# Operand placement in a two-layer encoder trunk: activations at one residue of 256 bytes, pair weights eight bytes further up, full-height decay products

## The chip, the core and the metric

The kernel runs on one core of a Trainium2 chip. The metric is device time in microseconds for one execution of the whole program, the median over several runs. A core has a matrix engine (TensorE, PE in the profile, with its weight loads listed apart as PEld), a vector engine (VectorE, DVE), an activation engine (ScalarE, ACT), a general engine (GpSimd, POOL), a queue engine (SyncE, SP), and 16 DMA engines that all queues share. Operands of a matrix product lie in SBUF, which has 128 partitions. A tile has the same byte address in each partition that it covers. This document is about those byte addresses, taken modulo 256.

## The reference

`x` is 512 frames by 1024 features, and there are two layers. One layer computes:

```
h = rmsnorm(x);  z = h @ w_in + b_in          # 12296 columns, split into parts
A: mLSTM, 4 heads:  s = (q k^T) * exp(log decay between frames), causal;  num = s @ v
   y_m = sigmoid(o) * head_norm(num / denominator)
B: retention, 4 heads:  s = (rope(q) rope(k)^T) * gamma^(distance), causal;  num = s @ v
   y_r = silu(g) * head_norm(num)
x += (sigmoid(gm) * (y_m @ w_bm) + sigmoid(gr) * (y_r @ w_br)) @ w_out
x += relu(rmsnorm(x) @ w_ff1 + b_ff1)^2 @ w_ff2 + b_ff2
x += sigmoid(rmsnorm(x) @ w_pe_gate) * (p @ w_pe)
```

A last rmsnorm ends the program. All of it is float32.

## The kernel before

Every float32 operand is held as two parts of TensorE's `float32r` type, a high and a low one, and a product is three matmuls into one accumulator: high by high, high by low, low by high (`mm3`, line 479). ScalarE writes the high part (line 303) and VectorE the low one (line 304); `split` does both. One matmul has 128 weight columns held in the array and streams 256 or 512 columns of the other operand past them. The text calls the streamed one the moving operand and the other the stationary one.

The work is cut into units, one list per layer (`unit_list`, line 171). Weights stream in with one DMA per unit or part of it, are split two pieces ahead of their use (`prep_next`, line 425; `LOOK`), and rotate through a pool `w`. There are three kinds of large unit.

- A T8 unit (`t8`, line 484): eight 128-row blocks of weights, stationary, against 512 columns of activations, 24 matmuls.
- A PAIR unit (`run_pair`, line 512): two output tiles by a fast 2x2 block scheme with seven products instead of eight. Each product is 12 matmuls of 256 moving columns at lines 531 to 533, so a unit has 84. Its weights are four pieces, A to D. Three of the seven moving operands are the activations themselves, four are sums of them, made ahead (`xs` from line 1329 for the mixing half of a layer, `ns` for the first feed-forward matrix). For the second feed-forward matrix all seven come from the `hid` tiles `h`. There are 75 PAIR units, so 6300 such matmuls: 32 units read `hid`, 28 read activations and `xs`, 15 read activations and `ns`.
- A WIDE unit (`run_wide`, line 549): the same scheme with the roles exchanged: weights are the moving operand, 512 columns, and activations or `xs` are stationary, at lines 575 to 577. There are eight, with 168 matmuls each; four sevenths of them, 768, have `xs` stationary.

The last seventh product of a PAIR unit (P4) is put off into the next unit (`later`, `flush`). The framework orders instructions on each engine by a priority and its own cost estimate, so rows of neighbouring products may interleave.

Where a tile lies is set by pools. `cpool` holds constants, among them `bc`, all bias and gain columns of both layers, loaded at the start. `pad` and the `shift` tiles (line 275) only take room, so that later tiles lie further up. With them, in the built program, all stationary weights begin at byte 224 of 256, and so do most activations; `xs`, `hid` and the operand `pt` begin at byte 32. One operand differs by head: an mLSTM value tile holds two heads of 258 columns, so in `attend` (line 830) the even heads' moving operand begins at byte 224 and the odd heads' at 232, against stationary operands at 224 for both. Each weight part, high and low, is a tile of its own, two tiles per piece (line 437).

The decay matrix of an mLSTM head starts from a product `rp` (line 1062): a selector `sel` and the gate rows `grows`, both 36 partitions high, spread one row over 128 partitions. There is one per head and layer, eight in all.

Of the kernel before, what the change touches and what calls it, by code (L numbers as in the profile page):

```python
# [35 lines left out]
F32 = mybir.dt.float32  # L36
F32R = mybir.dt.float32r
AF = mybir.ActivationFunctionType
OP = mybir.AluOpType
# [3 lines left out]
P = 128  # L43
T = 512
NT = T // P
D = 1024
KT = D // P
L = 2
H = 4
# [9 lines left out]
PIECES = 3  # L59
PAD = 48  # L60
LAST = 4
# [16 lines left out]

# [174 lines left out]
def build(ctx, tc, ins, out):  # L253
    nc = tc.nc
# [170 lines left out]
    def prep_next():  # L425
# [229 lines left out]
    class Norm:  # L655
# [10 lines left out]
        def col(self, k):  # L666
            o, _ = _B[self.gain]
            return bc[:, self.i, o + k:o + k + 1]

# [89 lines left out]
    def bcol(i, n, k):  # L759
        o, _ = _B[n]  # L760
        return bc[:, i, o + k:o + k + 1]

# [114 lines left out]
    def gate_rows(i, o, nrm):  # L877
# [42 lines left out]
        x = 0  # L920
# [42 lines left out]
    fill_raws(2)  # L963
    nc.scalar.dma_start(bc[:, 0, 8:NB], ins["vecs"][0][:, 8:NB])
    for k in range(1, KT):
# [6 lines left out]
    nc.sync.dma_start(ident, ins["ident"])  # L972
    nc.sync.dma_start(bc[:, 1, :], ins["vecs"][1])

    for i in range(L):
# [7 lines left out]

        sel = cur["br"].tile([P, H, P], F32R, name=f"l{i}sel", tag="sel")[0:32 + H]
        t = tmp(f"l{i}selraw")
        gp.memset(t[0:32 + H, :], 0.0)
        for r in (0, 32):
            nc.sync.dma_start(t[r:r + H, :T], ins["sel"])
        ve.tensor_copy(sel.rearrange("k h p -> k (h p)"), t[0:32 + H, :T])
        x_src = ins["xT"] if i == 0 else xs_dram  # L990
# [3 lines left out]
        negb = cols.tile([P, 16], F32, name=f"l{i}negb", tag="negb")  # L994
        gp.tensor_scalar(negb, bc[:, i, ob:ob + 16], -1.0, None, OP.mult)
        cbp = cols.tile([P, 16], F32, name=f"l{i}cbp", tag="cbp")
        gp.tensor_tensor(cbp, bc[:, i, ow:ow + 16], bc[:, i, ow + 16:ow + 32], OP.add)
        for j in (2, 3):
            gp.tensor_tensor(cbp, cbp, bc[:, i, ow + 16 * j:ow + 16 * j + 16], OP.add)
        gp.tensor_tensor(cbp, cbp, bc[:, i, ob:ob + 16], OP.mult)  # L1000
        gp.tensor_tensor(cbp, cbp, bc[:, i, oc:oc + 16], OP.add)

        fix = cols.tile([P, 3, 16], F32, name=f"l{i}fix", tag="fix", bufs=1)
        for j in range(3):
            gp.tensor_tensor(fix[:, 2 - j, :], bc[:, i, ow + 16 * j:ow + 16 * j + 16], negb, OP.mult)
            if j:
                gp.tensor_tensor(fix[:, 2 - j, :], fix[:, 2 - j, :], fix[:, 3 - j, :], OP.add)
# [16 lines left out]
        def conv_evac(o, nm, c, qh, ql, q, nrm):  # L1024
            a = tmp(f"{nm}cv")
            cw = [bc[:, i, ow + 16 * j + c:ow + 16 * j + c + 1] for j in range(4)]
            if nrm:
# [435 lines left out]
        for c in range(KT):  # L1463
# [118 lines left out]
        embed(1)  # L1582
        shift(cur["ff"], ph_side, False)
        cur["ff"].release()
# [142 lines left out]
def _pack_vecs(a):  # L1727
    v = np.zeros((L, P, NB), np.float32)
    for i in range(L):
        def put(n, x, off=0):  # L1730
            o, _ = _B[n]
            x = x.reshape(-1, P).T
            v[i, :, o + off:o + off + x.shape[1]] = x
# [11 lines left out]
        put("brk", b[CRK:CRK + 1024])  # L1745
        put("brg", b[CRG:CRG + 2048])
        put("bgm", b[CGM:CGM + 1024])
# [53 lines left out]
```

## Time and profile before

| what | value |
|---|---|
| median of three runs | 2320.76 us (lowest 2318.07) |
| the profiled execution: its span | 2313.4 us |
| outside the span, from the median | 7.4 us |
| PE busy | 2299.1 us, 13532 matmuls |
| PEld busy | 2035.4 us |
| DVE busy | 1766.8 us |
| ACT busy | 1269.6 us |
| POOL busy | 624.1 us |
| DMA | 499.36 MB, mean busy share by the page's rows about 0.8 |

The page gives busy time per engine. Matmuls are pipelined: one lasts longer in the record than the distance to the next, so a busy PE can still be slower than it need be. The measure that matters here is the spacing, the distance from one matmul's start to the next one's. It is read from the timeline, whose first column is the start in microseconds, the second the duration of one, and then the engine, the line, the operation, output<-inputs, and the shapes. The page's times are of one execution; the median is of others.

### The profile page before, as it was taken

The page shows a single profiled execution, that of the slowest core. Times are in us where ns is not written, and L with a number is a line of the kernel's source. Part 1 is how long each engine was busy: PE and PEld are TensorE (multiplying, and loading weights), DVE is VectorE, ACT ScalarE, POOL GpSimd, SP SyncE. Part 2 cuts the span into 40 slices and gives each one's busy share as a digit, 9 for nine tenths or more (in the row PEclk, how much of TensorE's full clock was granted, in tenths as well). Part 3 has the DMA queues.
Part 4 walks back from the last instruction along what each step waited for, and adds up shares of the span by engine and source line. Part 5 has one row for each costly group of instructions (what it writes and reads, how often), then busy time and mean ns, then how long its engine had stood idle before and what let it go on. Part 6 is the DMA issues. An engine that isn't in the chain of part 4 may idle for free.

```text
span 2313.4 us, 36468 instructions
## 1 busy us (share of the span) xinstructions
PE 2299.1 (99%) x13532; PEld 2035.4 (88%) x13532; DVE 1766.8 (76%) x2690; ACT 1269.6 (55%) x1837; POOL 624.1 (27%) x984
## 2 busy tenths in 40 slices
PE   9999999999999999999999999999999999999998
PEld 8888899888898899999888888988888888999997
DVE  7878767886676878788778777778867678787785
ACT  6756544644554546556557564445445446566564
POOL 4333222223124322223442332221231242111112
PEclk9999999999999999999999999999999999999999
DMA  7776787777789888888886768877877898878851
GB/s 218 189 191 174 238 228 216 215 227 210 232 230 261 220 228 223 240 239 215 222 224 182 196 174 247 232 216 216 223 221 208 241 266 218 247 232 228 232 160 55
DMA packets 187603, 499.36 MB, mean 216 GB/s; under 512 B 26064, under 2 KB 29520, under 8 KB 187424
## 3 DMA queue, kind: packets, MB, share of 16 engines
q0 software_dynamic: 57520, 188.53, 37.1%
q1 hardware_dynamic: 114496, 281.06, 36.6%
q10 hardware_dynamic: 15408, 27.43, 3.5%
q8 instruction: 106, 1.74, 0.3%
q14 instruction: 73, 0.60, 0.1%
HBM read 478.05 MB, written 194.51 MB: 291 GB/s over the span
## 4 chain that ended last, share of the span: by engine, by line
PE 92%; DVE 5%; ACT 1%; issue 1%; DMA 1%; POOL 0%; SPq 0%; ACTq 0%; DVEq 0%; POOLq 0%
PE l0br L480 1%; PE l1br L480 1%; PE l1br L481 1%; PE l0br L482 1%; PE l1br L482 1%; PE l0br L481 1%; PE l0f L480 1%; PE l0f L481 1%; PE l0f L482 1%; PE l1f L480 1%; PE l1f L481 1%; PE l1f L482 1%; PE l0pg L480 1%; PE l1bm L480 1%; PE l0pg L482 1%
## 5 line engine op out<-in xcount | busy, mean ns | idle before, releaser
L303 ACT ACTIVATE wh<-wr 128x1024 fp32r<-128x1024 f32 (+1 forms) x193 | 199.7, 1041 | 140.5 <-issue 17.1
L304 DVE TENSOR_TENSOR wl<-wr,wh 128x1024 fp32r<-128x1024 f32 (+1 forms) x191 | 234.6, 1230 | 37.5 <-ACT wh L303 36.9
L303 ACT ACTIVATE wh_B<-wr 128x1024 fp32r<-128x1024 f32 x123 | 130.3, 1059 | 184.5 <-PE l0br L481 15.7
L304 DVE TENSOR_TENSOR wl_B<-wr,wh_B 128x1024 fp32r<-128x1024 f32 x123 | 150.3, 1222 | 55.1 <-ACT wh_B L303 50.6
L303 ACT ACTIVATE wh_C<-wr 128x1024 fp32r<-128x1024 f32 x75 | 79.2, 1056 | 69.5 <-PE l0br L481 8.3
L304 DVE TENSOR_TENSOR wl_C<-wr,wh_C 128x1024 fp32r<-128x1024 f32 x75 | 91.7, 1223 | 21.3 <-ACT wh_C L303 17.1
L303 ACT ACTIVATE wh_A<-wr 128x1024 fp32r<-128x1024 f32 x75 | 78.9, 1052 | 44.3 <-DMA wr<-wpairs 5.2
L304 DVE TENSOR_TENSOR wl_A<-wr,wh_A 128x1024 fp32r<-128x1024 f32 x75 | 91.6, 1221 | 12.6 <-ACT wh_A L303 9.4
L303 ACT ACTIVATE wh_D<-wr 128x512 fp32r<-128x512 f32 x75 | 47.2, 630 | 96.5 <-DVE wr L462 27.3
L303 ACT ACTIVATE wh_t<-wr 128x1024 fp32r<-128x1024 f32 x56 | 59.4, 1061 | 69.0 <-PE l0g2va L576 6.0
L304 DVE TENSOR_TENSOR wl_t<-wr,wh_t 128x1024 fp32r<-128x1024 f32 x56 | 68.2, 1221 | 26.1 <-ACT wh_t L303 25.5
L304 DVE TENSOR_TENSOR wl_D<-wr,wh_D 128x512 fp32r<-128x512 f32 x75 | 51.8, 690 | 30.2 <-ACT wh_D L303 28.7
L480 PE MATMUL l0f<-l0n2h,wh 128*128 128x512 f32 x176 | 68.7, 390 | 0.0
L481 PE MATMUL l0f<-l0n2l,wh 128*128 128x512 f32 x176 | 68.6, 390 | 0.0
L482 PE MATMUL l0f<-l0n2h,wl 128*128 128x512 f32 x176 | 68.5, 389 | 0.0
L361 POOL DMA_DIRECT2D s30t<-wpairs x24 | 16.8, 699 | 92.4 <-PE l1o11a L533 9.4
L482 PEld LDWEIGHTS l0f<-l0n2h,wl 128*128 128x128 f32 x176 | 33.0, 188 | 7.0
L480 PEld LDWEIGHTS l0f<-l0n2h,wh 128*128 128x128 f32 x176 | 33.1, 188 | 6.6
L481 PEld LDWEIGHTS l0f<-l0n2l,wh 128*128 128x128 f32 x176 | 33.1, 188 | 6.5
L480 PE MATMUL l1f<-l1n2h,wh 128*128 128x512 f32 x96 | 37.6, 391 | 0.0
L481 PE MATMUL l1f<-l1n2l,wh 128*128 128x512 f32 x96 | 37.5, 390 | 0.0
L482 PE MATMUL l1f<-l1n2h,wl 128*128 128x512 f32 x96 | 37.4, 389 | 0.0
(5797 smaller groups left out, 9132.4 us busy)
## 6 DMA issues: line engine op xcount, KB each, us to landing
wr<-wstream SPq DMA_DIRECT2D x189, 512.0 KB, 4.8
wr<-wpairs SPq DMA_DIRECT2D x225, 256.0 KB, 4.1
wr<-wwide SPq DMA_DIRECT2D x48, 512.0 KB, 4.7
s3t<-wwide POOLq DMA_DIRECT2D x24, 256.0 KB, 5.0
s6t<-wwide POOLq DMA_DIRECT2D x24, 256.0 KB, 5.0
s18t<-wwide POOLq DMA_DIRECT2D x24, 256.0 KB, 4.7
s21t<-wwide POOLq DMA_DIRECT2D x24, 256.0 KB, 5.3
s24t<-wpairs POOLq DMA_DIRECT2D x24, 256.0 KB, 5.7
```

The costliest lines, as they stand in the source:

```text
L303: a = ac.activation(hi_ap, src, AF.Copy)
L304: return a, ve.tensor_sub(lo_ap, src, hi_ap.bitcast(F32))
L361: dma = gp.dma_start(piece(g, x, p, q), piece(g, MADE[x][a], p, q), max_dma_last_dim=4096, **kw)
L480: te.matmul(o, sh, mh, start=first, stop=False)
L481: te.matmul(o, sh, ml, start=False, stop=False)
L482: cur["mm"] = te.matmul(o, sl, mh, start=False, stop=last)
```

## The change

- `bc` keeps only the columns that are needed outside the branches (72 per layer instead of 249; the unused `brg` goes). The branch columns, 161 per layer, are a tile `bcl` loaded per layer by `branch_cols`: for layer 0 at the start, for layer 1 after the output projection of layer 0, both from ACT's queue.
- The `shift` tiles go. In the built program all moving and stationary activations, `xs`, `hid` and `pt` among them, now begin at byte 224.
- High and low part of a weight piece are slices of one tile, 64 columns longer than the two. In PAIR units, and in the four last units (whose matmuls have 256 columns), both parts begin two columns, 8 bytes, further in: at byte 232. The others stay at 224.
- `sel` and the gate rows are used at 128 partitions, with zeros below row 36, so `rp` is a 128-row product.

Number and shape of matmuls are otherwise the same.

```diff
-for _n, _c in (("g1", 8), ("g2", 8), ("g3", 8), ("gf", 8), ("bqk", 16), ("cw", 64), ("cb", 16), ("bo", 8),
-               ("brq", 8), ("brk", 8), ("brg", 16), ("bgm", 8), ("bgr", 8), ("bf1", 32), ("bf2", 8),
-               ("gmn", 8), ("grn", 16), ("bif", 1)):
+for _n, _c in (("g1", 8), ("g2", 8), ("g3", 8), ("gf", 8), ("bf1", 32), ("bf2", 8), ("bqk", 16), ("cw", 64), ("cb", 16),
+               ("bo", 8), ("brq", 8), ("brk", 8), ("bgm", 8), ("bgr", 8), ("gmn", 8), ("grn", 16), ("bif", 1)):
...
+NK = _B["bqk"][0]
+SLACK = 64
...
-    def shift(pl, side, start):
-
-        if (side == "left") == start:
-            pl.tile([P, 16 if start else 48], F32, name="shift", tag="shift")
...
-    bc = cpool.tile([P, L, NB], F32, name="bc")
+    bc = cpool.tile([P, L, NK], F32, name="bc")
     nc.scalar.dma_start(bc[:, 0, 0:8], ins["vecs"][0][:, 0:8])
+    bcl = {}
+
+    def branch_cols(i):
+
+        bcl[i] = cpool.tile([P, NB - NK], F32, name=f"bc{i}", tag="bcl")
+        nc.scalar.dma_start(bcl[i], ins["vecs"][i][:, NK:NB])
+
+    def bvec(i, o, n=1):
+        return bc[:, i, o:o + n] if o < NK else bcl[i][:, o - NK:o - NK + n]
...
-        kw = {"tag": "d", "bufs": 2} if x == "D" else {"tag": "l", "bufs": 2 * LAST} if pl is not wpool else {
-            "tag": "w", "bufs": 2 * PIECES}
+        kw = {"tag": "d", "bufs": 1} if x == "D" else {"tag": "l", "bufs": LAST} if pl is not wpool else {
+            "tag": "w", "bufs": PIECES}
...
-        out_ = [pl.tile([P, w], F32R, name=f"w{a}{n}_{nm}", **kw) for a in ("h" if gates else "hl")]
+        both = pl.tile([P, 2 * w + SLACK], F32R, name=f"w{n}_{nm}", **kw)
+        o = 2 if units[n][0] == "PAIR" or pl is not wpool else 0
+        out_ = [both[:, o + a * w:o + a * w + w] for a in range(1 if gates else 2)]
...
-        rr = cur["br"].tile([P, T], F32R, name=n + "rr", tag="rr")[0:32 + H]
+        rr = cur["br"].tile([P, T], F32R, name=n + "rr", tag="rr")
...
-    nc.scalar.dma_start(bc[:, 0, 8:NB], ins["vecs"][0][:, 8:NB])
+    nc.scalar.dma_start(bc[:, 0, 8:NK], ins["vecs"][0][:, 8:NK])
+    branch_cols(0)
...
-        sel = cur["br"].tile([P, H, P], F32R, name=f"l{i}sel", tag="sel")[0:32 + H]
+        sel = cur["br"].tile([P, H, P], F32R, name=f"l{i}sel", tag="sel")
...
-        shift(xs_pool, act_side, True)
         xs_t = acts(xs_pool, f"l{i}xs")
-        shift(xs_pool, act_side, False)
...
         cur["low"].release()
+        if i == 0:
+            branch_cols(1)
...
-        shift(cur["ff"], ph_side, True)
```

The framework also puts some rows in another order. On PE, at the gates of layer 0 after the first rope products, the old order ran the first matmul of the next product (output bank `l0bgm2b`) inside the product before it (`l0bgm2a`). `wh_B` and `wl_B` are the two parts of one weight piece, the same piece that is `w_B` now.

```order
L533 MATMUL l0r0brka<-l0xnh_1348,wl_D 128x256
L531 MATMUL l0bgm2a<-l0xsh_1373,wh_B 128x256
L532 MATMUL l0bgm2a<-l0xsl_1374,wh_B 128x256
L531 MATMUL l0bgm2b<-l0xnh_1059,wh_B 128x256
L533 MATMUL l0bgm2a<-l0xsh_1373,wl_B 128x256
```

Now, from the same place:

```order
L541 MATMUL l0r0brka<-l0xnh_1331,w_D 128x256
L539 MATMUL l0bgm2a<-l0xsh_1356,w_B 128x256
L540 MATMUL l0bgm2a<-l0xsl_1357,w_B 128x256
L541 MATMUL l0bgm2a<-l0xsh_1356,w_B 128x256
L539 MATMUL l0bgm2a<-l0xsh_1360,w_B 128x256
```

The matmul that reads the low part (line 533, now 541) moves one place forward, and the borrowed matmul goes back into its own product.

On POOL, the derived convolution columns of layer 1 (`l1negb`, `l1cbp`, `l1fix`) stood near the program's start, since `bc` held both layers:

```order
L1000 TENSOR_TENSOR l0cbp<-l0cbp,bc 128x16
L1001 TENSOR_TENSOR l0cbp<-l0cbp,bc 128x16
L995 TENSOR_SCALAR l1negb<-bc 128x16
L997 TENSOR_TENSOR l1cbp<-bc 128x16
L999 TENSOR_TENSOR l1cbp<-l1cbp,bc 128x16 x2
```

Now they stand at the end of layer 0's mixing half, among the DMAs that fetch `x` again and those that make the weight sums `s10t` for the second feed-forward matrix:

```order
L1453 DMA l0x_7212<-xT 128x512
L367 DMA s10t_120<-wpairs 64x1024
L1004 TENSOR_SCALAR l1negb<-bc_7621 128x16
L1006 TENSOR_TENSOR l1cbp<-bc_7621 128x16
L1014 TENSOR_TENSOR l1fix<-bc_7621,l1negb 128x16 x2
L1008 TENSOR_TENSOR l1cbp<-l1cbp,bc_7621 128x16
```

There `l1negb` waits until the second load of branch columns has landed, and the weight sums behind it wait with it.

More of the change, by code (lines that the diff above doesn't have):

```diff
@@ L667, in col @@
             o, _ = _B[self.gain]
-            return bc[:, self.i, o + k:o + k + 1]
+            return bvec(self.i, o + k)
         def tile(self, k, x):
@@ L760, in bcol @@
         o, _ = _B[n]
-        return bc[:, i, o + k:o + k + 1]
+        return bvec(i, o + k)
     def rows_split_v(i, h, nm, n_, j, o, rc, bvt, vh, vl):
@@ L972, in build @@
     nc.sync.dma_start(ident, ins["ident"])
-    nc.sync.dma_start(bc[:, 1, :], ins["vecs"][1])
+    nc.sync.dma_start(bc[:, 1, :], ins["vecs"][1][:, 0:NK])
     for i in range(L):
@@ L994, in build @@
         negb = cols.tile([P, 16], F32, name=f"l{i}negb", tag="negb")
[L995 removed]
+        gp.tensor_scalar(negb, bvec(i, ob, 16), -1.0, None, OP.mult)
         cbp = cols.tile([P, 16], F32, name=f"l{i}cbp", tag="cbp")
[L997 removed]
+        gp.tensor_tensor(cbp, bvec(i, ow, 16), bvec(i, ow + 16, 16), OP.add)
         for j in (2, 3):
[L999 to L1001 removed]
+            gp.tensor_tensor(cbp, cbp, bvec(i, ow + 16 * j, 16), OP.add)
+        gp.tensor_tensor(cbp, cbp, bvec(i, ob, 16), OP.mult)
+        gp.tensor_tensor(cbp, cbp, bvec(i, oc, 16), OP.add)
         fix = cols.tile([P, 3, 16], F32, name=f"l{i}fix", tag="fix", bufs=1)
         for j in range(3):
[L1005 removed]
+            gp.tensor_tensor(fix[:, 2 - j, :], bvec(i, ow + 16 * j, 16), negb, OP.mult)
             if j:
@@ L1025, in conv_evac @@
             a = tmp(f"{nm}cv")
-            cw = [bc[:, i, ow + 16 * j + c:ow + 16 * j + c + 1] for j in range(4)]
+            cw = [bvec(i, ow + 16 * j + c) for j in range(4)]
             if nrm:
@@ L1582, in build @@
         embed(1)
-        shift(cur["ff"], ph_side, False)
         cur["ff"].release()
@@ L1745, in _pack_vecs @@
         put("brk", b[CRK:CRK + 1024])
-        put("brg", b[CRG:CRG + 2048])
         put("bgm", b[CGM:CGM + 1024])
```

4 lines of the change are left out of this document (2 added, 2 removed).

## The prediction

> **What bounds the kernel now.** I read the page's busy times and chain first, then windows for counts, then the timeline of TensorE for spacings.
>
> ```profile
> span 2313.4 us, 36468 instructions
> PE 2299.1 (99%) x13532; PEld 2035.4 (88%) x13532; DVE 1766.8 (76%) x2690; ACT 1269.6 (55%) x1837; POOL 624.1 (27%) x984
> PEclk9999999999999999999999999999999999999999
> PE 92%; DVE 5%; ACT 1%; issue 1%; DMA 1%; POOL 0%; SPq 0%; ACTq 0%; DVEq 0%; POOLq 0%
> ```
>
> TensorE is the bound: busy for 99% of the span, 92% of the chain, granted clock at full throughout. So the time is a sum of spacings between matmul starts plus a few waits. What matters is whether spacing depends on where operands lie. Rows of three PAIR products, the first and the twelfth matmul of each, eleven spacings apart:
>
> ```profile
> 992.79 0.28 PE L531 MATMUL l0o20b<-l0hh,wh_B 128*128 128x256 f32 x1
> ...
> 994.09 0.28 PE L533 MATMUL l0o20b<-l0hh,wl_B 128*128 128x256 f32 x1
> ...
> 1002.78 0.28 PE L531 MATMUL l0o21b<-l0hh,wh_B 128*128 128x256 f32 x1
> ...
> 1004.03 0.28 PE L533 MATMUL l0o21b<-l0hh,wl_B 128*128 128x256 f32 x1
> ...
> 1027.34 0.28 PE L531 MATMUL l0f31c<-l0nsh,wh_A 128*128 128x256 f32 x1
> ...
> 1028.66 0.28 PE L533 MATMUL l0f31c<-l0nsh,wl_A 128*128 128x256 f32 x1
> ```
>
> 1.30/11 is 118 ns with the moving operand at byte 32 (`l0hh`), 1.32/11 is 120 ns at byte 224 (`l0nsh`), where stationary and moving operand agree; weights are at 224 in both. The middle product is as the first in addresses, but takes 1.25/11, 113.6 ns. So there is a faster state, and it lasts:
>
> ```profile
> 995.30:1025.80 30.50, 30.50 (x272) 30.50 (x271) 25.86 (x42) 12.45 (x14) 5.97 (x9) 1.00 0.92 254
> 1983.80:2007.10 23.30, 23.30 (x208) 23.30 (x208) 18.63 (x30) 8.70 (x10) 2.90 (x4) 1.00 0.88 245
> ```
>
> (columns: window, its length, PE busy and count, then PEld, DVE, ACT, POOL, clock, DMA share, GB/s). Without the three matmuls that were already in flight at each start, 30.50/269 is 113.4 ns and 23.30/205 is 113.7 ns. I take 113.4 as the floor for 256 columns.
>
> Now the 512-column matmuls: a T8 unit, and a WIDE unit with first activations and then `xs` stationary.
>
> ```profile
> 342.56 0.39 PE L480 MATMUL l0bm<-l0ymh,wh 128*128 128x512 f32 x1
> ...
> 347.77 0.39 PE L482 MATMUL l0bm<-l0ymh,wl 128*128 128x512 f32 x1
> ...
> 403.71 0.40 PE L575 MATMUL l0g0va<-wh_B,l0xnh 128*128 128x512 f32 x1
> ...
> 409.18 0.40 PE L575 MATMUL l0g0vc<-wh_t,l0xsh 128*128 128x512 f32 x1
> ...
> 414.78 0.40 PE L575 MATMUL l0g0va<-wh_t,l0xsh 128*128 128x512 f32 x1
> ```
>
> T8, all at 224: 5.21/23 = 226.5 ns. WIDE, all at 224: 5.47/24 = 227.9 ns. WIDE with `xs` at byte 32: 5.60/24 = 233.3 ns. At 512 columns equal residues are the good case, at 256 the bad one.
>
> **The change, part by part.** *Pairs.* Of 6300 matmuls 4032 have the moving operand at byte 32 and 2268 at 224 (units and operands as listed above). Some 475 of the first kind run at 113.4, the rest at 118; the second kind at 120. The sum is 475 x 113.4 + 3557 x 118 + 2268 x 120 = 745.8 us, a mean of 118.4 ns. After the change the moving operand is at 224 and the weights at 232, a pairing that no PAIR unit of before has. Its bounds are rows of the trace. Below, the floor, 113.4: 6300 x 5.0 = 31 us won. Above, the spacing of a pair stream that has just changed state:
>
> ```profile
> 1699.59 0.29 PE L531 MATMUL l1r3brkb<-l1xnh,wh_B 128*128 128x256 f32 x1
> 1699.72 0.28 PE L532 MATMUL l1r3brkb<-l1xnl,wh_B 128*128 128x256 f32 x1
> 1699.84 0.29 PE L533 MATMUL l1r3brkb<-l1xnh,wl_B 128*128 128x256 f32 x1
> ```
>
> up to 130 ns, 6300 x 11.6 = 73 us lost. The nearest row is the mLSTM attend, 258 columns: even heads with both operands at 224, odd heads with the moving one 8 bytes further up.
>
> ```profile
> 94.33 0.28 PE L480 MATMUL l0m0a<-l0m0vh,l0m0ph 128*128 128x258 f32 x1
> ...
> 97.80 0.28 PE L482 MATMUL l0m0a<-l0m0vh,l0m0pl 128*128 128x258 f32 x1
> ...
> 141.44 0.28 PE L480 MATMUL l0m1a<-l0m0vh,l0m1ph 128*128 128x258 f32 x1
> ...
> 144.89 0.28 PE L482 MATMUL l0m1a<-l0m0vh,l0m1pl 128*128 128x258 f32 x1
> ```
>
> 3.47/29 = 119.7 ns against 3.45/29 = 119.0. Eight bytes help there by 0.7 ns, with the shift on the other operand and a length that is no multiple of 256 bytes, so that the pattern never settles. With 256 columns each matmul repeats the last one's addresses, and a good phase, once reached, can stay, as the two long windows show. I choose the floor for most of it: a stream that at 120 and 118 keeps to one spacing over whole products depends on a phase between the two reads, and 8 bytes on one of them change that phase. This is the weakest choice of the sum. The Trainium skill ("TensorE: Matmul & The Clock Gate", Back-to-back issue gap) states a lower floor than these rows, N/2.4 + 2.5 ns: an estimate of 109.2 ns for 256 columns and 215.8 for 512, against 113.4 and 226.5 here; by it the pairs would win 58 us.
>
> *Last units.* Their 192 matmuls of 256 columns get the same offset; at 120 now, by the mean of the l0f31c rows, 192 x 6.6 = 1.3 us.
>
> *WIDE.* 768 matmuls with `xs` at 32 go to 224: 768 x (233.3 - 227.9) = 4.1 us won, up to 5.2 if they reach 226.5. The `pt` units (96 matmuls of 512 columns) are too few to count.
>
> *Decay products.* The 36-row product, its neighbour before and after:
>
> ```profile
> 68.15 0.50 PE L1062 MATMUL l0m0rp<-l0grr,l0sel 36*128 36x512 f32 x1
> 68.58 0.50 PE L480 MATMUL l0m0s<-l0m0qh,l0m0kh 128*128 128x512 f32 x1
> 68.92 0.39 PE L481 MATMUL l0m0s<-l0m0ql,l0m0kh 128*128 128x512 f32 x1
> ```
>
> 0.77 us for two matmuls that at 226.5 would take 0.45: 0.32 us, eight times, 2.5 us. No 128-row pair of equal kind in the rows above shows such a gap, so I take all of it; the bound is 0, if the gap comes from the switch of operands.
>
> *Branch columns.* At the start ACT's queue issues one DMA more:
>
> ```profile
> 1.72 0.45 ACTq L964 DMA_DIRECT2D bc<-vecs  x1
> 3.63 1.28 ACT L676 ACT_TABLE_LOAD   x1 [3.63 <-DMA x<-xT]
> ```
>
> 0.45 us, inside the 1.46 us that ACT waits for `x` from 2.17 to 3.63; without that cover the start would be 0.45 us later. The second load is another 0.45 us on ACT, which is busy 55%, ahead of weight splits that run two pieces ahead. On POOL `l1negb` waits there for the landing, a few microseconds (the first `x` in the row above took until 3.63); queued behind it are weight sums for the second feed-forward matrix, which is multiplied only in the next half of the layer. POOL is busy 27%. I cost both at nothing.
>
> *Halves in one tile.* A slot is free when both parts have been read, one matmul later for the high part: 0.1 to 0.2 us on a split made two pieces ahead. Nothing, or at the few places where TensorE waits for VectorE already, that much. At the gates `l0bgm2` in the rows above, the matmul that needs the low part comes one earlier: 0.12 us more wait.
>
> *What is late next.* VectorE. Around the waits it is full:
>
> ```profile
> 988.00:998.00 10.00, 9.77 (x80) 9.35 (x79) 10.00 (x16) 6.86 (x8) 2.10 (x3) 1.00 0.94 236
> 1085.00:1100.00 15.00, 14.86 (x126) 14.60 (x125) 14.58 (x23) 7.35 (x10) 5.97 (x7) 1.00 0.92 233
> ```
>
> PAIR stages that run 4% faster get nothing from it in such stretches: about 0.4 us in each 10. With some eight of them (one per second feed-forward block and one at each layer's rope) I take 3 us back.
>
> **Sum.** 31 + 1 + 4 + 2.5 - 3 = 35.5 us, from 2313.4 to 2278 us of span. The median lies 7.4 us over the profiled span, so 2320.8 - 35.5 = **2285 us**, 1.5% faster.
>
> **Rivals.**
>
> *Eight bytes do as little as in the odd heads.* Pairs settle at 120 - 0.7 = 119.3, against 118.4 now: 5.7 us lost, while the rest wins 6.6: 2320 us. For it: the one pair of rows with that offset. Against: the length.
>
> *Residues decide nothing; the state does.* The rows for it are l0o20b and l0o21b: equal residues, 118 and 113.6. Only the decay products change: 2318 us. Against it stand 233.3 and 227.9 within one WIDE unit. The Trainium skill ("SBUF — State Buffer", Who interferes with whom) gives TensorE independent read ports for the two operands, and says it never waits on anyone; by that rule addresses should not matter. The trace disagrees by 5.4 ns a matmul.
>
> *VectorE takes the gain.* Windows that hold a VectorE-full stretch grow with every us that TensorE saves; if half of the PAIR time is like that, 16 us of the 31 go: 2301 us. Against: VectorE is at 25.86 of 30.50 us in the window at 113.4, with no wait.
>
> *Slower: the new pairing is the worst phase.* If pairs keep a spacing of the changing stream, the mean of the 0.13 and 0.12 above, 125 ns, they lose 6300 x 6.6 = 42 us, less 5 from the rest: 2358 us, 1.6% slower. It decides from 118.4 + 6.6/6.3 = 119.5 ns on; over 2% takes 126.8 ns or more. Against it: no row keeps such a spacing over a product.
>
> *Faster still: the floor falls too.* If 113.4 is itself a phase, pairs could go below it; at 111.7 ns they win 42 us and the sum passes 46. Against it: 269 and 205 matmuls in a row that stay at 113.4 to 113.7, and T8 at 226.5, twice 113.25. A page's lower floor (above, the Trainium skill) would give 2258 us; no row here comes near it.
>
> **How the numbers follow.** 2%, 46 us, is about what a measurement of this kernel tells from no change. The forecast has 0.50; VectorE or half-reached pairs (2292 to 2312) 0.17; the two rivals at about 2320 together 0.25; slower by the phase 0.05; the lower floor 0.03. The range reaches from a forecast without the 3 us and with WIDE at its best, 2281, less 2 for the distance between the lowest run and the median, to the rivals at 2320: 0.47 and 0.17 and most of 0.25. Over 2% faster is the lower floor alone: 0.03. Over 2% slower: 0.03. Within: 0.94.
>
> **What would show it.** In the changed kernel's timeline, PAIR products of `l0f`, `l0o` and the rope units alike at 1.25 us for eleven spacings; WIDE products alike at 5.45 to 5.47 us for 24; `rp` followed 0.23 us later by the scores; the waits of TensorE no longer than before but for some tenths at VectorE's full stretches. PAIR products at 118 to 120, or differing between products of one unit, would make the forecast wrong, and a new wait behind POOL's `l1negb` or ACT's load would show as a gap at the end of layer 0's mixing half.

## The result and the profile after

The changed kernel takes 2302.02 us (median) against 2319.67 us for the kernel before in the same session: ratio 0.9928, 95% interval 0.9912 to 0.9945. That is 17.65 us faster, 0.7%, a small gain but clear of no change. Each median counts one execution of four that ran far slower (4679.1 us before, 3239.82 us after, this one at a granted clock of 0.654); without them the medians are 2318.58 and 2301.85 us, 16.7 us apart, and the ratio is theirs. The forecast was 2285 us, 35.5 us faster: half of it came.

The page of the changed kernel, first its span, then busy time by engine, then the chain that ended last:

```profile
span 2300.5 us, 36407 instructions
PE 2277.2 (99%) x13532; PEld 2020.8 (88%) x13532; DVE 1759.0 (76%) x2690; ACT 1266.5 (55%) x1835; POOL 616.2 (27%) x984
PE 85%; DVE 7%; ACT 2%; issue 2%; DMA 2%; POOL 1%; SPq 0%; DVEq 0%; ACTq 0%; POOLq 0%
```

TensorE's share of the chain fell from 92% to 85%, and VectorE's rose from 5% to 7%. So matmuls became cheaper, and waits longer. Both can be read from rows. First the timeline of a PAIR product (`l0f31c` again, first and twelfth matmul), then one window that holds PAIR products alone (columns as in the prediction):

```profile
1022.10 0.28 PE L539 MATMUL l0f31c<-l0nsh,w_A 128*128 128x256 f32 x1
...
1023.37 0.28 PE L541 MATMUL l0f31c<-l0nsh,w_A 128*128 128x256 f32 x1
991.00:1018.00 27.00, 27.00 (x236) 27.00 (x235) 22.40 (x37) 10.06 (x11) 5.96 (x9) 1.00 0.86 242
```

1.27/11 = 115.5 ns, where before it was 120. In the window 27.00/233 (without three in flight at its start) is 115.9 ns. Every PAIR unit runs so: neither 118 nor 120 any more, but not 113.4 either. The prediction's own sign, 1.25 us for eleven spacings, came as 1.27.

A WIDE unit with `xs` stationary, the first matmul of a product and the first of the next, 24 further on, and the decay product with its neighbours:

```profile
406.46 0.39 PE L583 MATMUL l0g0vc<-w_t,l0xsh 128*128 128x512 f32 x1
...
411.90 0.39 PE L583 MATMUL l0g0va<-w_t,l0xsh 128*128 128x512 f32 x1
69.43 0.39 PE L1071 MATMUL l0m0rp<-l0grr,l0sel 128*128 128x512 f32 x1
69.66 0.39 PE L488 MATMUL l0m0s<-l0m0qh,l0m0kh 128*128 128x512 f32 x1
69.88 0.39 PE L489 MATMUL l0m0s<-l0m0ql,l0m0kh 128*128 128x512 f32 x1
```

5.44/24 = 226.7 ns, from 233.3; and `rp` now takes 0.23 us to the next start, with no gap behind it.

The waits of TensorE (what waited, on what, microseconds in total, times, longest), some of those that the kernel before does not have or has shorter:

```profile
PE l0gr0a L539 <- ACT l0gr0y L610: 1.1, 1, 1.1
PE l0if L1026 <- ACT l0n1h L684: 1.0, 1, 1.0
PE l1r2vc L584 <- DVE w_t L310: 0.8, 1, 0.8
PE l1f10a L541 <- DVE w_B L310: 0.8, 1, 0.8
PE l0r2vc L584 <- DVE w_t L310: 0.8, 1, 0.8
PE l0r2vc L583 <- ACT w_t L309: 0.7, 1, 0.7
PE l1r2vc L583 <- ACT w_t L309: 0.7, 1, 0.7
PE l0o10a L539 <- DVE l0x L1531: 0.5, 1, 0.5
```

To weigh the two sides I went through the starts of all matmuls of both traces. Where a spacing is over 35 ns longer than 113.4 ns (256 columns) or 226.5 ns (512), the excess is counted as a pause of TensorE, and the mean spacings leave that spacing out.

| term | forecast, us | from the two traces, us |
|---|---|---|
| PAIR, 6300 matmuls | +31 (118.4 to 113.4 ns) | +15.5 (118.20 to 115.74 ns) |
| last units, 192 | +1.3 | +0.8 (119.9 to 115.7) |
| 512 columns | +4.1 | +6.7: `xs` 768 x (233.3 - 226.9) = 4.9, the rest small gains of the others |
| decay products | +2.5 | +2.1 (pauses 2.5 to 0.35) |
| other pauses | -3 | -12.5 (14.2 to 26.7) |
| sum | 35.5 | 12.6 (the spans differ by 12.9) |

The table explains the two profiled spans, 12.9 us apart; the times differ by 16.7. Over 45 executions of the kernel before, in the four later sessions, the span runs from 2312.9 to 2319.5 us with a median of 2316.3, so the profiled one, 2313.4, was a short one, by some 3 us. What made it short is open. In these executions the time is 1.7 us above the span, so most of the 7.4 us that stand above as "outside the span" is the distance between two executions.

The other pauses by place, in us before and after: start 0.6 and 2.0, WIDE 0.7 and 4.7, gates of the retention output and of `bgm` 1.4 and 3.9, feed-forward 5.4 and 11.2, the rest 6.0 and 4.8.

### The profile page after: what moved, and what is told of

It reads as the page before. It is cut to its first block, busy times and chain, and to the rows that moved or that the text cites. A ratio compares the mean times of both kernels' runs of the same rounds, so it can differ in the third digit from the quotient of the medians.

```text
span 2300.5 us, 36407 instructions
## 1 busy us (share of the span) xinstructions
PE 2277.2 (99%) x13532; PEld 2020.8 (88%) x13532; DVE 1759.0 (76%) x2690; ACT 1266.5 (55%) x1835; POOL 616.2 (27%) x984
## 4 chain that ended last, share of the span: by engine, by line
PE 85%; DVE 7%; ACT 2%; issue 2%; DMA 2%; POOL 1%; SPq 0%; DVEq 0%; ACTq 0%; POOLq 0%
PE l0f L488 1%; PE l0f L489 1%; PE l0f L490 1%; PE l0br L488 1%; PE l1br L488 1%; PE l1br L490 1%; PE l0br L490 1%; PE l1br L489 1%; PE l0br L489 1%; DVE w_B L310 1%; PE l1f L488 1%; PE l1f L490 1%; PE l1f L489 1%; DVE w_C L310 1%; PE l0pg L488 1%
## 5 line engine op out<-in xcount | busy, mean ns | idle before, releaser
L309 ACT ACTIVATE w<-wr 128x1024 fp32r<-128x1024 f32 (+1 forms) x193 | 199.7, 1042 | 125.9 <-issue 28.5
L310 DVE TENSOR_TENSOR w<-wr,w 128x1024 fp32r<-128x1024 f32 (+1 forms) x193 | 233.8, 1214 | 45.3 <-ACT w L309 44.7
L309 ACT ACTIVATE w_B<-wr 128x1024 fp32r<-128x1024 f32 x123 | 130.4, 1060 | 150.5 <-PE l0bm L490 13.1
L310 DVE TENSOR_TENSOR w_B<-wr,w_B 128x1024 fp32r<-128x1024 f32 x123 | 150.0, 1221 | 55.0 <-ACT w_B L309 54.5
L309 ACT ACTIVATE w_C<-wr 128x1024 fp32r<-128x1024 f32 x75 | 79.3, 1057 | 66.8 <-issue 9.6
L310 DVE TENSOR_TENSOR w_C<-wr,w_C 128x1024 fp32r<-128x1024 f32 x75 | 92.4, 1233 | 25.0 <-ACT w_C L309 21.0
L309 ACT ACTIVATE w_A<-wr 128x1024 fp32r<-128x1024 f32 x75 | 79.0, 1054 | 46.6 <-DMA wr<-wpairs 4.4
L310 DVE TENSOR_TENSOR w_A<-wr,w_A 128x1024 fp32r<-128x1024 f32 x75 | 91.6, 1222 | 14.2 <-ACT w_A L309 12.0
L309 ACT ACTIVATE w_D<-wr 128x512 fp32r<-128x512 f32 x75 | 47.3, 631 | 81.6 <-DVE wr L470 26.7
L488 PE MATMUL l0f<-l0n2h,w 128*128 128x512 f32 x176 | 68.7, 390 | 0.0
L490 PE MATMUL l0f<-l0n2h,w 128*128 128x512 f32 x176 | 68.5, 389 | 0.0
L488 PE MATMUL l1f<-l1n2h,w 128*128 128x512 f32 x96 | 37.6, 391 | 0.0
L490 PE MATMUL l1f<-l1n2h,w 128*128 128x512 f32 x96 | 37.4, 390 | 0.0
```

What stands on the lines that cost most here:

```text
L309: a = ac.activation(hi_ap, src, AF.Copy)
L310: return a, ve.tensor_sub(lo_ap, src, hi_ap.bitcast(F32))
L488: te.matmul(o, sh, mh, start=first, stop=False)
L490: cur["mm"] = te.matmul(o, sl, mh, start=False, stop=last)
```

## The experiments

There are two questions: why PAIR stopped at 115.7 ns, and where 12.5 us of pauses came from. Theory 1: 8 bytes have a spacing of their own, and one tile for both halves, costed at nothing, moves ScalarE's splits. Rivals: another offset holds 113.4; the pauses come from the load of the branch columns; a faster TensorE waits for VectorE whatever is done. In the table, pauses and mean spacings are worked out from all starts, as above, each from one profiled execution; the pauses include those at the decay products. The rows come from five sessions, so ratios, each against the kernel before in the same session, compare better than times.

| kernel | time, us | ratio, 95% interval | PAIR, ns | pauses, us |
|---|---|---|---|---|
| before | 2317.6 to 2319.8 | | 118.2 | 16.7 |
| changed | 2302.02 | 0.9928, 0.9912 to 0.9945 | 115.7 | 27.0 |
| no 8 bytes | 2323.08 | 1.0024, 1.0015 to 1.0034 | 119.9 | 20.7 |
| no 8 bytes, own tiles | 2317.38 | 0.9997, 0.9987 to 1.0006 | 119.9 | 14.2 |
| before, one tile | 2324.17 | 1.003, 1.002 to 1.004 | 118.4 | 22.7 |
| changed, late columns | 2301.53 | 0.9931, 0.9916 to 0.9946 | 115.7 | 25.6 |
| changed, 36 rows | 2305.41 | 0.9939, 0.9922 to 0.9955 | 115.7 | 32.0 |
| 64 bytes | 2305.96 | 0.9945, 0.993 to 0.996 | 116.1 | 24.9 |
| own tiles, 8 bytes | 2299.24 | 0.9917, 0.9902 to 0.9932 | 115.7 | 20.1 |
| the same, late columns | 2297.41 | 0.991, 0.9895 to 0.9925 | 115.7 | 19.5 |
| the same again | 2298.43 | 0.9909, 0.9892 to 0.9925 | 115.7 | 21.1 |
| own tiles, late columns, 64 bytes, 4-column products | 2299.74 | 0.9915, 0.9901 to 0.993 | 115.4 | 24.1 |

### Many offsets in one kernel

```diff
-        o = 2 if units[n][0] == "PAIR" or pl is not wpool else 0
+        same = [k for k, u in enumerate(units) if u[0] == units[n][0]]
+        o = 0 if gates else OFFS[same.index(n) % len(OFFS)]   # 0,1,2,3,4,5,6,8,12,16,24,32,40,48,56
```

> The changed kernel, but each unit puts both parts of its weights at another offset: 0, 1, 2, 3, 4, 5, 6, 8, 12, 16, 24, 32, 40, 48 or 56 columns of 4 bytes, in turn, for each kind of unit. Only the spacing by offset is read, not the time. If the spacing is set by the distance of the two operands' addresses: PAIR units at 0 columns show 119.9 ns, at 2 columns 115.7, at 16 or 48 columns (64 bytes up or down) 117.7, and some offset reaches 113.4 in all its units. If it is set by the state the stream is in alone: units of one offset differ among themselves as much as units of different offsets, with some at 113.4 and some at 118 to 120 for the same offset. For 512 columns the first theory expects 226.5 ns at 0 columns and more, up to 233, at 16 columns.

One execution, 2339.11 us. Mean spacing of PAIR units by offset, some 415 matmuls each, and the range over the means of the five units of an offset (in the range, without the seventh product, which runs within the next unit):

| columns (bytes) | ns | units | | columns (bytes) | ns | units |
|---|---|---|---|---|---|---|
| 0 (0) | 119.7 | 119.6 to 119.9 | | 12 (48) | 118.1 | 117.8 to 119.4 |
| 1 (4) | 118.3 | 118.2 to 118.3 | | 16 (64) | 115.1 | 113.5 to 117.8 |
| 2 (8) | 115.9 | 115.7 to 116.0 | | 24 (96) | 118.8 | 117.3 to 120.1 |
| 3 (12) | 116.6 | 116.6 to 116.7 | | 32 (128) | 118.9 | 118.6 to 120.1 |
| 4 (16) | 118.4 | 118.3 to 118.4 | | 40 (160) | 119.8 | 119.6 to 120.0 |
| 5 (20) | 118.5 | 117.9 to 120.0 | | 48 (192) | 116.7 | 113.4 to 117.8 |
| 6 (24) | 120.1 | 118.7 to 121.8 | | 56 (224) | 117.1 | 116.6 to 117.8 |
| 8 (32) | 118.3 | 118.2 to 118.5 | |  | |  |

No offset holds 113.4 in every unit. Eight bytes have one spacing, 115 to 117 ns from matmul to matmul. Two offsets have units at 113.4 to 113.5 and units at 117.8: 64 bytes, and 192, which is how `hid` and the weights stood to each other before (224 - 32). So the fast state that the prediction saw belonged to that distance. It is the distance, and not where the weights alone lie: at 192 the weights begin at byte 160 here and began at byte 224 before, and both show the two spacings. For 512 columns equal residues are best: WIDE, one unit for each offset, 227.2 ns at 0, and 229.0 to 239.5 ns at seven other offsets.

### The 8 bytes taken away

```diff
-        o = 2 if units[n][0] == "PAIR" or pl is not wpool else 0
+        o = 0
```

> The changed kernel without the 8 bytes: all weight parts at byte 224. If the 8 bytes alone brought the pairs from 118.4 to 115.7 ns, all pairs now take 119.9: 6492 matmuls by 4.2 ns are 27 us more spacing. If the changed kernel's longer waits (27 us of gaps over 35 ns against 17 before) come from VectorE that cannot follow faster pairs, they fall back to about 15 us and the time is 2302 + 27 - 11 = 2318 us. If the longer waits come from the rows' order, which the one tile per weight piece changed, they stay near 27 and the time is 2329 us.

2323.08 us, ratio 1.0024. PAIR runs at 119.9 ns. The product whose rows stand above, `l0f31c`, first and twelfth matmul, takes 1.32/11 = 120 ns:

```profile
1028.98 0.28 PE L539 MATMUL l0f31c<-l0nsh,w_A 128*128 128x256 f32 x1
...
1030.30 0.28 PE L541 MATMUL l0f31c<-l0nsh,w_A 128*128 128x256 f32 x1
```

So the offset is worth 4.2 ns a matmul, some 27 us in 6492 (the last units have it too), and gives 21 us of time against the changed kernel. Pauses fall from 27.0 to 20.7 us, neither to 15 nor to 27 as the two readings had it, and the time lies between theirs: both causes have a part. Without the offset the rest of the change loses, though `xs` and the decay products have their gains: the pauses at WIDE are there too (6.8 us), and pairs at one residue cost 1.7 ns more than the 118.2 of before, 11 us.

### One tile per piece in the kernel before

```diff
-        out_ = [pl.tile([P, w], F32R, name=f"w{a}{n}_{nm}", **kw) for a in ("h" if gates else "hl")]
+        both = pl.tile([P, 2 * w], F32R, name=f"w{n}_{nm}", **kw)
+        out_ = [both[:, a * w:a * w + w] for a in range(1 if gates else 2)]
```

> The kernel before, with high and low part of a weight piece as slices of one tile, and nothing else: addresses, shift tiles, columns and decay product as before. If VectorE's lag behind faster pairs makes the longer waits: pairs are as before, waits stay at 17 us, and the time at 2319.7 (within 1 us). If one tile per piece reorders the splits: the two waits of 0.9 and 1.0 us at the third WIDE unit of each layer appear here too, waits grow to 21 to 25 us, and the time is 2324 to 2328 us.

2324.17 us, ratio 1.003 (1.002 to 1.004): the shared tile by itself costs 7 us. Pauses grow by 6.0 us (WIDE +3.9, feed-forward +3.0, gates +1.7, the other places 2.6 less). The units at distance 192 now run at 117.8 ns but for a few in part (two have means below 117), where eight had run wholly or partly at 113.4 before: their mean rises from 116.9 to 117.7 ns, some 2 us in 2688 matmuls. Whether that share of fast units changes from one execution of a kernel to the next, which could also make an execution short, no second trace of the kernel before can tell.

### Own tiles again, without the 8 bytes

```diff
-        both = pl.tile([P, 2 * w + SLACK], F32R, name=f"w{n}_{nm}", **kw)
-        o = 2 if units[n][0] == "PAIR" or pl is not wpool else 0
-        out_ = [both[:, o + a * w:o + a * w + w] for a in range(1 if gates else 2)]
+        out_ = [pl.tile([P, w], F32R, name=f"w{a}{n}_{nm}", **kw) for a in ("h" if gates else "hl")]
```

(with twice as many slots, as before)

> The changed kernel with the 8 bytes taken away and the two halves of a piece in tiles of their own again; branch columns, decay products on 128 rows and the one residue stay. With shared tiles and without the 8 bytes the time was 2323.1 us. Theory 1 (one tile for both halves costs some 6.5 us: ScalarE gets its splits in a later place, behind an activation that waits for GpSimd): 2316.5 us, and the gaps of 0.9 and 1.0 us ahead of l0r2vc and l1r2vc are gone. Rival (these gaps come from the branch columns or from the new residues): 2323 us with the gaps still there.

2317.38 us, as theory 1 said (2316.5), 5.7 us less than with the shared tile (ratios 0.9997 and 1.0024, their intervals apart); pauses fall from 20.7 to 14.2 us. The mechanism stands in ScalarE's timeline. First the changed kernel, then TensorE at the same place:

```profile
455.03 0.72 ACT L1200 ACTIVATE l0g0y<-l0g0y,l0r1hv 128x512 f32<-128x512 f32 x1 [3.70 <-POOL l0r1hv L1158]
455.66 1.99 ACT L309 ACTIVATE w_t<-wr 128x1024 fp32r<-128x1024 f32 x2
```

```profile
455.63 0.39 PE L585 MATMUL l0r2vc<-w_t,l0xsl 128*128 128x512 f32 x1
456.75 0.51 PE L583 MATMUL l0r2vc<-w_t,l0xsh 128*128 128x512 f32 x1 [0.74 <-ACT w_t L309]
458.01 0.50 PE L584 MATMUL l0r2vc<-w_t,l0xsh 128*128 128x512 f32 x1 [0.75 <-DVE w_t L310]
```

And ScalarE with tiles of their own:

```profile
452.20 1.06 ACT L309 ACTIVATE wh_t<-wr 128x1024 fp32r<-128x1024 f32 x1
456.92 0.72 ACT L1198 ACTIVATE l0g0y<-l0g0y,l0r1hv 128x512 f32<-128x512 f32 x1 [3.66 <-POOL l0r1hv L1156]
457.55 1.05 ACT L309 ACTIVATE wh_t<-wr 128x1024 fp32r<-128x1024 f32 x1
```

ScalarE stands 3.7 us at an activation that waits for GpSimd. With own tiles one split is done ahead of it; with the shared tile the framework's order puts it behind, and TensorE waits 0.9 us for the high part and 1.0 for the low one, in both layers. A likely reason, not shown, is that six slots of single halves can be handed out as each comes free, and three joint ones only when both halves are. Giving the high and low halves three slots each, on tags of their own, also leaves the split behind the activation in the built order (that version has no run): in this order two pools of three do not do what one of six does.

### Branch columns later

```diff
-    branch_cols(0)
     for k in range(1, KT):
         nc.sync.dma_start(x[k], ins["xT"][k])
...
     nc.sync.dma_start(ident, ins["ident"])
+    branch_cols(0, nc.sync)
```

> The changed kernel with layer 0's branch columns loaded on SP's queue after the x tiles instead of on ACT's ahead of them. If that load delays the x tiles at the start: ACT gets its second x tile at 6.9 us instead of 8.3, the gaps of TensorE before 12 us fall from 2.0 to 0.6 us, and the time from 2302.0 to 2300.6 us. If x was late for another reason: the gaps and 2302.0 stay.

2301.53 us against 2302.02: no difference that the intervals show. In the changed kernel's profile SyncE's seven `x` transfers took long to issue, and the second one arrived late; the kernel without the 8 bytes has the same start:

```profile
2.22 6.16 SPq L975 DMA_DIRECT2D x<-xT  x7
8.31 0.72 ACT L684 ACTIVATE l0n1h<-x,bc 128x512 fp32r<-128x512 f32 x1 [1.98 <-DMA x<-xT]
```

```profile
2.18 4.82 SPq L975 DMA_DIRECT2D x<-xT  x7
6.45 0.72 ACT L684 ACTIVATE l0n1h<-x,bc 128x512 fp32r<-128x512 f32 x1
```

8.31 us there, 6.45 here (before 6.90, late 7.35). The kernel without the 8 bytes also has the extra transfer ahead of `x`, and 0.1 us of pauses at the start. So the 1.4 us more that the changed kernel's profile has there were mostly that execution's, not the extra transfer's.

### Decay products on 36 rows again

```diff
-        rr = cur["br"].tile([P, T], F32R, name=n + "rr", tag="rr")
+        rr = cur["br"].tile([P, T], F32R, name=n + "rr", tag="rr")[0:32 + H]
-        sel = cur["br"].tile([P, H, P], F32R, name=f"l{i}sel", tag="sel")
+        sel = cur["br"].tile([P, H, P], F32R, name=f"l{i}sel", tag="sel")[0:32 + H]
```

> The changed kernel with the decay products on 36 rows again, all else as changed. Forecast's reading: each of the eight products costs TensorE 0.32 us beside it, 2.5 us in all: 2304.5 us, with gaps ahead of and behind the eight rows of l0m0rp to l1m3rp. Rival (the pauses stand beside a wait that is there anyway): 2302 us, no difference.

2305.41 us; the ratios differ by 0.0011, 2.6 us, though their intervals overlap. The trace has the gaps back, 2.5 us against 0.35, at the rows named:

```profile
69.01 0.50 PE L1071 MATMUL l0m0rp<-l0grr,l0sel 36*128 36x512 f32 x1
69.44 0.50 PE L488 MATMUL l0m0s<-l0m0qh,l0m0kh 128*128 128x512 f32 x1
69.77 0.39 PE L489 MATMUL l0m0s<-l0m0ql,l0m0kh 128*128 128x512 f32 x1
```

0.76 us for two spacings, as before. (Its 32 us of pauses hold 3.7 us more at WIDE than the changed kernel's profile, at the same instructions: such pauses differ between executions by some microseconds.)

### 64 bytes for 8

```diff
-        o = 2 if units[n][0] == "PAIR" or pl is not wpool else 0
+        o = 16 if units[n][0] == "PAIR" or pl is not wpool else 0
```

> The changed kernel with the pairs' split weights 64 bytes further up in place of 8. Forecast's reading (a product of 256 columns can start every 113.4 ns once its weights stand where they do not meet the moving operand, and 8 bytes was only not the best place): in the look at many offsets single units ran at 113.4 ns here; if all do, 6492 products save 2.3 ns each, 15 us, 2287 us. Rival (no offset holds 113.4 ns through a whole unit, the state changes from unit to unit): mean 115.2 to 116.5 ns, 2299 to 2307 us.

2305.96 us, ratio 0.9945 against 0.9928, some 4 us more than 8 bytes, though the intervals overlap. PAIR has a mean of 116.1 ns, a mixture, as the rival said. Two units of this one trace, `l0gr2` and `l0o22`, alike in residues:

```profile
683.02 0.28 PE L539 MATMUL l0gr2a<-l0xsh,w_B 128*128 128x256 f32 x1
...
684.91 0.28 PE L540 MATMUL l0gr2b<-l0xnl,w_B 128*128 128x256 f32 x1
1006.10 0.28 PE L539 MATMUL l0o22a<-l0hh,w_B 128*128 128x256 f32 x1
...
1008.70 0.28 PE L541 MATMUL l0o22b<-l0hh,w_B 128*128 128x256 f32 x1
```

1.89/16 = 118 ns and 2.60/23 = 113 ns. Followed from start to start, a run of PAIR products keeps its spacing until TensorE pauses, and after a pause it may have the other one: the spacing changes 20 times in this trace, each time within some matmuls of a spacing of 144 ns or more. All 29 runs of PAIR units that follow products of other units begin at 117.4 to 118.0 ns. So there are two states at one placement, and a run keeps the one that it begins with: the forecast's reading, that a good phase, once reached, stays, holds here, but it took reaching it for granted.

### A small product to set the state

Own tiles and late columns as further below, 64 bytes, and at the first matmul of each of these 29 runs one of seven forms of a small product:

```diff
+                if kick == "f32":
+                    te.matmul(o[:, 0:2], ones, ones[:, 0:2], start=True, stop=True, ...)
+                elif kick == "two":      # the first product in two of 128 columns
+                    ...
+                elif kick:               # 4, 32, 64, 128 or 192 columns
+                    te.matmul(o[:, 0:kick], wh[:, s], h[:, 0:kick], start=True, stop=True, ...)
```

> Own tiles for the two halves, branch columns late, pairs 64 bytes up as in the run with 64 bytes, where each run of pairs kept one of two spacings, 113.4 or 117.8 ns, from its first product to the next pause of TensorE, and nearly every unit that followed products of 512 columns began in the slow one. Here each such unit begins with one small product more, whose result is overwritten (4, 32, 64, 128 or 192 columns in float32r, 2 columns in float32), or with its first product cut into two of 128 columns, one of the seven forms by turns. Theory (the spacing is a phase between reading weights and reading the moving operand, set when the run begins): some of the forms put the whole unit at 113.4 ns, the same form alike at each place where it stands; others leave it at 117.8 ns. Rival (the state comes from something else, such as which transfers run): the forms make no difference, units behind 512 columns stay near 117.8 ns, and each small product costs its own time alone.

Of 29 runs 27 now begin at 113.3 to 114.3 ns; the other two, at 117.8, both with 32 columns, which worked at two other places. `l0gr2` again, with the product of 4 columns ahead of it:

```profile
676.76 0.17 PE L552 MATMUL l0gr2a<-l0xnh,wh_A 128*128 128x4 f32 x1
676.79 0.36 PE L554 MATMUL l0gr2a<-l0xnh,wh_A 128*128 128x256 f32 x1
...
677.22 0.28 PE L554 MATMUL l0gr2a<-l0xnh,wh_A 128*128 128x256 f32 x1
...
678.47 0.28 PE L556 MATMUL l0gr2c<-l0xsh,wl_A 128*128 128x256 f32 x1
```

1.25/11 = 114 ns, at a cost of 0.12 us (0.03 for itself, and 0.20 in place of 0.113 to the next start). (Some forms change what their units sum, so this kernel leaves out part of the reference's result.) A gain in time is not shown: 2298.82 us in one execution. PAIR falls to a mean of 114.5 ns, 7.9 us less than in the same kernel with 8 bytes, and pauses rise by 6.9 us, of which about half are the small products themselves (29 x 0.12).

With the form of 4 columns at every place:

> As the kernel of seven small products, with the 4-column form at every place: pairs 64 bytes up, and each unit of a pair that follows other products begins with one product of 4 columns that is overwritten. Theory 1 (the phase set at the beginning holds): nearly every product of a pair at 113.4 ns, a mean near 113.9. What this is worth: if TensorE sets the pace, 6400 x (115.7 - 113.9) = 11.5 us less, and 32 x 0.12 = 3.8 us more for the small products, so 7 to 8 us below the same kernel with 8 bytes, near 2290 us. Theory 2 (the chains of VectorE and ScalarE set the pace of the pairs' units): the gaps ahead of the pairs grow by most of it, 2295 to 2299 us. Rival (the phase was chance): mean 116 ns as with 64 bytes alone, 2302 us or more.

2299.74 us against 2298.43 for the kernel with 8 bytes in the same session. 23 of the 29 runs begin fast; the six that do not are the four that follow products of 256 columns (`l0r1`, `l0r3`, `l1r1`, `l1r3`) and the two at `gr0`. At four of these six places (`l0r1`, `l0r3`, `l1r1`, `l1gr0`) the run began fast in the kernel of seven forms, behind another form and with nothing else changed. So the product ahead, and not the tiles of their own (no run has these with 64 bytes and no small product), set how these runs began. Why one form works at a place and another does not is open. Waits inside the feed-forward part change the state again, and in the end 53% of the products are at 113 to 115 ns, a mean of 115.4. Theory 1 holds for how most runs begin, not for the mean expected of it (113.9), and no time is won. What 113.4 throughout would give has not been measured.

### Own tiles and 8 bytes

```diff
+        out_ = [pl.tile([P, w + SLACK], F32R, name=f"w{a}{n}_{nm}", **kw)[:, o:o + w] for a in ("h" if gates else "hl")]
...
-        vh = [cur["low"].tile([P, 576], F32R, name=f"{nm}vh{j}", tag="vh", bufs=NT) for j in range(NT)]
+        vh = [cur["low"].tile([P, 544], F32R, name=f"{nm}vh{j}", tag="vh", bufs=NT) for j in range(NT)]
```

(`vl` and `ml` alike, `bcl` in `low`, and `PAD` 88 for 48, which keeps the residues of PAIR and WIDE)

> The changed kernel with the two halves in tiles of their own, each with the slack, so the pairs keep the 8 bytes; the room comes from narrower value tiles (544 columns for 576, which moves every second one by 128 bytes; some 190 products are read from there) and from branch columns that lie with the phase's temporaries. Theory 1 (sharing the tile costs 6.5 us of gaps, the pairs keep 115.7 ns): 2295.5 us. Rival (the gaps are what a faster TensorE waits for anyway, VectorE and ScalarE set the pace): 2301 to 2302 us, the gaps only move.

2299.24 us. Pauses 20.1 us; those ahead of `l0r2vc` and `l1r2vc` are gone, as theory 1 said. But it forecast 2295.5, and the rival 2301 to 2302. What did not come is in the pauses: without the 8 bytes own tiles have 14.2 us of them, with them 20.1, of which the feed-forward part has 7.7 for 3.8. And the narrower value tiles cost 0.9 us in the 480 products that read them.

Four kernels now show each cost twice. Sharing a tile adds 6.5 us of pauses without the 8 bytes (14.2 to 20.7) and 6.9 with them (20.1 to 27.0). The 8 bytes add 5.9 us with own tiles and 6.3 with shared ones (20.7 to 27.0), where nothing else differs; of the 6.3 the feed-forward part has 4.7, and the start, where executions differ, 1.9. With neither, the pauses outside the decay products are 13.9 us, as in the kernel before (14.2), so the two make up the 12.5 us. In time the shared tile shows clearly only without the 8 bytes: with them the ratios, 0.9928 and 0.9917, have intervals that overlap.

> As the kernel with halves in tiles of their own and the 8 bytes, and layer 0's branch columns fetched by SyncE behind the tiles of x. Theory (the extra transfer at the start costs 1.0 us): 1.0 us below that kernel, near 2294.5 us, and the first two gaps of TensorE shorter by 1 us together. Rival (the start is hidden by a later wait, as one run suggested): no difference.

2297.41 us, ratio 0.991. Against the changed kernel's 0.9928 that is 0.0018 less, some 4 us, with intervals that overlap; against own tiles alone it is 1.8 us, within the intervals. The same kernel again, in the session of the small products:

> The kernel with own tiles for the halves, 8 bytes, and late branch columns once more, on the same chip as the one with the 4-column products, so that the two can be compared: 2297 us, with pairs at 115.7 ns.

2298.43 us, 0.9909. Both say the same, and no version here is faster. Its waits of TensorE in the feed-forward part:

```profile
PE l0o10a L542 <- DVE l0x L1533: 0.5, 1, 0.5
PE l0o20a L542 <- DVE l0x L1533: 0.5, 1, 0.5
PE l1o32a L542 <- DVE l1x L1533: 0.4, 1, 0.4
```

These remain with own tiles. Why, the kernel before shows beside the changed one: TensorE at `l0o10a`, and VectorE, before and then after.

```profile
908.57 0.28 PE L533 MATMUL l0o10c<-l0hh,wl_A 128*128 128x256 f32 x1
908.96 0.36 PE L531 MATMUL l0o10a<-l0hh,wh_B 128*128 128x256 f32 x1
908.40 0.41 DVE L1523 TENSOR_TENSOR l0x<-l0x,l0o10a 128x256 f32<-128x256 f32 x1
```

```profile
903.36 0.28 PE L541 MATMUL l0o10c<-l0hh,w_A 128*128 128x256 f32 x1
904.14 0.36 PE L539 MATMUL l0o10a<-l0hh,w_B 128*128 128x256 f32 x1 [0.51 <-DVE l0x L1531]
902.45 1.22 DVE L310 TENSOR_TENSOR w_B<-wr,w_B 128x1024 fp32r<-128x1024 f32 x1
903.58 0.41 DVE L1531 TENSOR_TENSOR l0x<-l0x,l0o10a 128x256 f32<-128x256 f32 x1
```

VectorE goes from the split of `w_B` to `l0x` without a break, and TensorE needs the bank that `l0x` empties. Measured from the start of `l0x`, the last matmul ahead came 0.17 us after it before and 0.22 us ahead of it now: TensorE came 0.4 us sooner, and the spacing there grew by 0.4 us (0.39 to 0.78). At the other feed-forward places the wait is on the same row by the list, and was not followed so.

## Why the prediction was wrong

**Wrong: the price of PAIR.** The step that failed is "I choose the floor for most of it", called there the weakest choice: 6300 x 5.0 = 31 us. Measured, 8 bytes have a spacing of their own, 115.7 ns, so the term is 15.5 us, half of its size. The 113.4 of the two long windows belonged to units at another distance, 192 bytes, which has two states, 113.3 and 118; what 8 bytes do could not be read from them. The bounds (113.4 and 130) held the value. The nearest row, the odd heads, gave 119.0 and was no guide either: it has 258 columns, and the shift on the other operand. (That its pattern never settles is the prediction's guess; no run shows it.) The case that came, "half-reached pairs (2292 to 2312)", had 0.17 together with VectorE.

**Wrong: one tile at nothing.** The step "a slot is free when both parts have been read, one matmul later" priced the tile's release, and not what the framework does with it: it set ScalarE's split behind an activation that waits 3.7 us. It costs 6.5 us of pauses without the 8 bytes and 6.9 with them, and 7 us of time in the kernel before. The rows of the order were there to be read ahead; the prediction read those of TensorE and GpSimd, not ScalarE's.

**Right in kind, too small: VectorE.** The prediction took 3 us back. Faster PAIR products cost some 6 us of pauses: 6.3 with shared tiles, and 5.9 with own tiles (where the narrower value tiles and the moved `bcl` lie in it), 4.7 and 3.8 of them in the feed-forward part. The rival "VectorE takes the gain", whose 2301 us is next to the result, came by its number through half a gain at PAIR and half of its own mechanism: it supposed 16 us taken, and they were 6. That is luck.

**Right.** TensorE is the bound, and spacing depends on where operands lie. `xs` at 224: 4.9 us for 4.1. Decay products: 2.1 us in the trace for 2.5; in time about 2.6, within the intervals. GpSimd's `l1negb` held up nobody: no pause over 0.12 us stands between the retention gates of layer 0 and its feed-forward products. The extra transfer at the start has no cost that was measured. The offset wins, so the rival that 8 bytes do as little as in the odd heads (2320 us) and that of the worst phase (2358 us) fall.

**Half right: the state.** The rival "residues decide nothing; the state does" falls, since offsets differ by up to 5 ns; but at 64 and at 192 bytes the state decides between 113.3 and 118. The Trainium skill ("SBUF — State Buffer", Who interferes with whom) gives TensorE independent read ports for its two operands and has it wait on nobody. What the prediction made of it, that addresses should not matter, is not so here: the sweep has 115.9 to 120.1 ns with nothing moved but the weights by a few bytes. Why the distance sets the spacing, no run here shows.

## What to carry to other kernels

A spacing seen at one distance between operands is no price for another. Let one kernel use many offsets, unit by unit, and read off the spacing, and whether it is the same in all units, before all units are moved. A tile that joins two buffers can cost more than its release. Where a framework orders by readiness, compare the order of the engine that fills it, with the waits of the rows it now stands behind. Of a faster bound engine expect only part: where it waits for an engine that works without a break, the wait can grow by what the matmuls save, as at `l0o10a` (0.4 us for 0.4).

## What was not expected of the hardware

- Matmuls of 256 float32r columns have a spacing that depends on the distance of weights and moving operand modulo 256 bytes, and at some distances there are two lasting spacings, 113.3 and 117.8 ns, with nothing else changed. A run keeps one until TensorE pauses; at 64 bytes 29 of 29 runs behind other products began slow, and 27 of 29 fast when one of seven forms of a small product stood ahead (23 with the 4-column form alone).
- What suits 256 columns does not suit 512: at equal residues 119.7 and 227.2 ns, at 8 bytes 115.9 and 233.6, at 20 bytes 118.5 and 239.5 (WIDE, one unit each).
- No unit has a mean below 113.3 ns (256 columns) or 226.7 ns (512) in any trace. The Trainium skill ("TensorE: Matmul & The Clock Gate", Back-to-back issue gap) states N/2.4 + 2.5 ns for an isolated matmul, an estimate of 109.2 and 215.8 ns; no run here reached it.
- The pauses of one kernel differ between executions: at WIDE 4.7 us in the changed kernel's profile, 8.4 with only the decay products undone. So the pauses of one trace do not explain a difference of 2 us between kernels.
